# Unused bytes ahead of six SBUF pools of a three-layer transformer kernel

## The chip, the cores and the metric

One core of one Trainium2 chip runs the program. The time is the device time of one execution in microseconds; of several runs the median is taken.

## What is computed

A sequence of 512 tokens with 1,024 features goes through two layers of a first block and one of a second, all in float32. Cut to its outline:

```python
def first_block(x, ...):
    for layer in range(2):
        h = _rms_norm(x, norm_mix_pre[layer])
        m = _even_mixer(h, ...) if layer % 2 == 0 else _odd_mixer(h, ...)
        x = x + _rms_norm(m, norm_mix_post[layer])
        h = _rms_norm(x, norm_ffn_pre[layer])
        f = _conv_ffn(h, ...)          # gate, val = split(h @ w_up); (gelu(conv(gate)) * val) @ w_down
        x = x + _rms_norm(f, norm_ffn_post[layer])
    return x

def second_block(x, ...):
    x = x + gated_deltanet(rms_norm(x, norm_mix[0]), ...)
    x = x + squared_relu_mlp(rms_norm(x, norm_mlp[0]), ...)   # square(relu(h @ w_up)) @ w_down
    return rms_norm(x, norm_final)
```

The even mixer has eight heads of attention with a forget gate and eight of latent attention; the odd mixer has eight heads of differential attention; the DeltaNet is a gated delta rule in chunks of 64. Each mixer ends in a product with a 1024x1024 matrix `w_out`. The FFN is 2,816 wide, the MLP 4,096.

## The kernel before

A float32 product is computed as three products of parts. Every activation and every weight `v` is split into `hi` (rounded to the type float32r) and `lo = v - hi`, and `mm3` (lines 173 to 175) adds `hi*hi`, `hi*lo` and `lo*hi` in one PSUM bank:

```python
mm(out, lhs[0], rhs[0], start=start, stop=False)
mm(out, lhs[0], rhs[1], start=False, stop=False)
return mm(out, lhs[1], rhs[0], start=False, stop=stop)
```

`lhs` is the operand that is loaded into TensorE (128 columns of 4 bytes, 512 bytes of a partition); `rhs` streams past it (512 columns, 2,048 bytes). In the trace's names `out<-rhs,lhs` the streaming operand comes first.

Weights come in tiles of 128x1024: SyncE's queue loads `raw` (`wload`, line 153), ScalarE writes `whi` (line 168), VectorE or GpSimd `wlo` (line 169). The pool `wp` holds two `raw`, four `whi` and four `wlo`. The normed input of a layer lies transposed in `hhi` and `hlo` (pool `hp`). Two forms of product occur. In the first the weights are loaded and the activations stream (`step_A`: tiles `gate`, `val`, `up`, `dproj`, `kq`, `fkq`, `uq`, `kn`, `head`). In the second the activations are loaded and the weights stream (`proj_B`: `tok`, `headb`, `z`, `c`, `mv`; and `Out.mm`: `o`).

`Out` and `proj_out` compute the product that ends each mixer, FFN and half of the MLP. Its activation parts are `fhi`/`flo` and `mhi`/`mlo` (even mixer), `ahi`/`alo` (FFN), `ohi`/`olo` (odd mixer), `gp0` to `gp3` (DeltaNet) and `mhi`/`mlo` (MLP). For each 128 rows of the weight the loop goes over two halves of 512 columns and four token tiles, so that eight PSUM banks called `o` are filled, three matmuls in a row to a bank. The last four weight tiles (the tail) are taken token tile by token tile, so that norm and transposition (`pn_t`) of the next layer can begin; the order there is written by hand (`manual_schedule`), as it is in the two attention mixers.

Pools are opened and closed in program order, and a pool's tiles lie one behind the other in SBUF in the order in which they are first made. A tile that takes bytes which an earlier tile had waits for the earlier one's readers (`reuse_waits="tile"`). `conv_ffn` first makes `cw` (352 bytes of a partition) and loads it through SyncE's queue (line 1178), then makes `ahi` and `alo`.

Of the kernel before, what the change touches and what calls it, by code (L numbers as in the profile page):

```python
# [10 lines left out]
F32 = mybir.dt.float32  # L11
# [10 lines left out]
P = 128  # L22
# [42 lines left out]
def parts(hi, lo):  # L65

    return lambda k, t: (hi[:, k, t * P:(t + 1) * P], lo[:, k, t * P:(t + 1) * P])


class Kern:  # L70
# [41 lines left out]

    def pool(self, name, **kw):
        return self.tc.tile_pool(name=name, bufs=1, reuse_waits="tile", **kw)

    def ps(self, tag, name="ps"):

        return self.psum.tile([P, 512], F32, tag=tag, name=name, bufs=2)
# [323 lines left out]
    def even_mixer(self, gain_post, nxt):  # L442
        nc, a = self.nc, self.a
        with self.pool("ev_o") as op_:

            fox = op_.tile([P, 4, S], F32R, name="fhi"), op_.tile([P, 4, S], F32R, name="flo")
            oT = op_.tile([P, 4, S], F32, name="oT")
            act = [parts(*fox), None]
            out = Out(self, lambda k, t: act[k // 4](k % 4, t), 8, lambda k: a["ev_wout"][k])
            with self.pool("ev") as pp, self.smalls(pp):  # L450
                self._even_attention(pp, fox, oT, out)
            with self.pool("ev_w") as wo:
                mla = wo.tile([P, 4, S], F32R, name="mhi"), wo.tile([P, 4, S], F32R, name="mlo")
                act[1] = parts(*mla)
                for c in range(4):
                    self.split(mla[0][:, c, :], mla[1][:, c, :], oT[:, c, :])
                self.proj_out(out, self.postnorm_add(gain_post), nxt)

    def _even_attention(self, pp, fox, oT, out):
# [25 lines left out]


        qs, q2, k2 = [pp.tile([P, 2, S], F32R, tag=n, name=n) for n in ("qs", "q2", "k2")]
        cT = (pp.tile([P, 5, S], F32R, name="chi"), pp.tile([P, 5, S], F32R, name="clo"))
        low = (cT[0][:, 0:2, :], cT[0][:, 2:4, :]), (q2, k2)
        for q2, k2 in low:  # L490
# [378 lines left out]
    def odd_mixer(self, gain_post, nxt):  # L869
        nc, a = self.nc, self.a  # L870
        with self.pool("od_o") as op_:
            ohi = op_.tile([P, 8, S], F32R, name="ohi")
            olo = op_.tile([P, 8, S], F32R, name="olo")
            with self.pool("od") as pp, self.smalls(pp):
                out = Out(self, parts(ohi, olo), 8, lambda k: a["od_wout"][k])
                self._odd_attention(pp, ohi, olo, out)
            self.proj_out(out, self.postnorm_add(gain_post), nxt)
# [296 lines left out]
    def conv_ffn(self, l, gain_post, nxt):  # L1174
        nc, a = self.nc, self.a
        with self.pool(f"ff{l}") as pp:
            cw = pp.tile([P, NFF, 4], F32, name="cw")
            nc.sync.dma_start(cw, a["ff_conv"][l])
            ahi = pp.tile([P, NFF, S], F32R, name="ahi")
            alo = pp.tile([P, NFF, S], F32R, name="alo")  # L1180
            for j in range(NFF):
                if j == 0:
                    first = self.head_rest()
                if j < 2:
                    pg, pv = first[2 * j:2 * j + 2]
                else:
                    pg, pv = self.ps("a", "gate"), self.ps("b", "val")
                    for i, ps in enumerate((pg, pv)):
                        self.proj_A(ps, self.wtile(a["ff_wup"][l, 2 * j + i]), P, KC, self.hT)
                c = pp.tile([P, S], F32, tag="cv", name="cv", bufs=2)  # L1190
                nc.scalar.activation(c, pg, AF.Identity, bias=cw[:, j, 3:4], scale=cw[:, j, 2:3])
                for sft in (1, 2):
                    nc.vector.scalar_tensor_tensor(c[:, sft:], pg[:, :S - sft], cw[:, j, 2 - sft:3 - sft], c[:, sft:],
                                                   ALU.mult, ALU.add)
                nc.scalar.activation(c, c, AF.Gelu_apprx_tanh)
                nc.vector.tensor_tensor(c, c, pv, ALU.mult)
                self.split(ahi[:, j, :], alo[:, j, :], c)

            self.proj_out(Out(self, parts(ahi, alo), NFF, lambda k: a["ff_wdown"][l, k]), self.postnorm_add(gain_post), nxt)


    def deltanet(self, nxt):
        nc, a = self.nc, self.a
        self.spill_x()
        with self.pool("dn_o") as op_:

            wq = [op_.tile([P, 8, 4, 64], F32, tag=f"wq{t}", name=f"wq{t}") for t in range(NT)]
            new_parts = lambda t: op_.tile([P, 2, 8, P], F32R, tag=f"wq{t}", name=f"gp{t}")
            nw = op_.tile([P, 1], F32, name="dnw")
            nc.sync.dma_start(nw, a["dn_nw"])  # L1210
            with self.pool("dn") as pp, self.smalls(pp):
                hd = [dict(h=h, wq=[w[:, h] for w in wq]) for h in range(8)]
                with self.pool("dn_t") as tp:
                    st = {}
                    gates = self._dn_gates(tp, pp, st)
                    next(gates)
                    for n in ("lk", "lrho", "nk", "ikd"):
                        st[n] = pp.tile([P, 8, NT], F32, name="d" + n)

                    st["u"] = pp.tile([P, NT, 8, P], F32, name="u")  # L1220
                    st["rq"] = pp.tile([P, NT, 8], F32, name="rq")
                    for d in hd[:KA]:
                        self._dn_kq(tp, st, d)
                    for _ in gates:
                        pass
                    for h in range(8):
                        if KA <= h + 1 < 8:
                            self._dn_kq(tp, st, hd[h + 1])
                        self._dn_qk(tp, pp, st, hd[h])
                    solve = self._dn_solve(tp, st)  # L1230
                    next(solve)
                    for d in hd:
                        self._dn_v(tp, pp, st, d)
                        for _ in range(4):
                            next(solve, None)
                    for _ in solve:
                        pass
                with self.pool("dn_s") as sp:
                    out = self._dn_tail(sp, pp, st, hd, new_parts, nw)
            self.reload_x()  # L1240

            self.proj_out(out, self.plain_add(), nxt)
# [429 lines left out]
    def mlp(self, nxt):  # L1672
        nc, a = self.nc, self.a
        with self.pool("mlp") as pp:
            for part in range(2):
                hi = pp.tile([P, 16, S], F32R, tag="mhi", name="mhi", bufs=1)
                lo = pp.tile([P, 16, S], F32R, tag="mlo", name="mlo", bufs=1)
                for j in range(0, 16, 2):
                    if part + j == 0:
                        first = self.head_rest()  # L1680
                    if part == 0 and j < 4:
                        pss = first[j:j + 2]
                    else:
                        pss = [self.ps("ab"[i], "up") for i in range(2)]
                        for i, ps in enumerate(pss):
                            self.proj_A(ps, self.wtile(a["ml_wup"][part * 16 + j + i]), P, KC, self.hT)
                    for i in range(2):
                        r = pp.tile([P, S], F32, tag="relu", name="relu", bufs=3)
                        nc.scalar.activation(r, pss[i], AF.Relu)
                        nc.vector.tensor_tensor(r, r, r, ALU.mult)  # L1690
                        self.split(hi[:, j + i, :], lo[:, j + i, :], r)

                self.proj_out(Out(self, parts(hi, lo), 16, lambda k: a["ml_wdown"][part * 16 + k]), self.plain_add(),
                              nxt if part else None)
# [191 lines left out]
```

## Time and profile before

| | |
|---|---|
| median of 3 runs | 1962.18 us (1961.23 to 1965.1) |
| profiled execution, its own time | 1961.64 us |
| its span | 1959.9 us |
| granted TensorE clock, mean | 0.999 |
| TensorE busy | 1929.2 us, 98% of the span, 9,960 matmuls |
| weight loads | 1583.7 us, 81% |
| VectorE / ScalarE / GpSimd busy | 1012.9 / 819.2 / 253.2 us |
| DMA | 177.76 MB, mean 91 GB/s |

The span runs from the first to the last instruction of the profiled execution; the execution's own time is 1.74 us longer. Matmuls are pipelined: a matmul's duration in a row reaches from its start to its modelled end, and the next one starts long before that end. Busy time is the union of these durations.

### The profile page before, as it was taken

Reading aid. Unit: us, or ns where it says so; the run is one execution under the profiler, and the core shown is the slowest. Engines: PE = TensorE matmul, PEld = TensorE weight load, DVE = VectorE, ACT = ScalarE, POOL = GpSimd, SP = SyncE. Lnnn points to the kernel's source line nnn. Section 1 sums busy time; section 2 is a strip of 40 time slices with the busy share of each in tenths; the row PEclk is TensorE's granted clock in tenths of the full one; section 3 lists DMA queues with packets and bytes.
Section 4 is the critical chain, followed back from the end, with each engine's and each line's share of the span. In section 5 each row is a group of like instructions: output and inputs, shape, how many; then the busy total and the mean of one; then the engine's idle time right before and its main releaser. Section 6 shows DMA issues by size and latency. Waiting matters only on the chain.

```text
span 1959.9 us, 25300 instructions
## 1 busy us (share of the span) xinstructions
PE 1929.2 (98%) x9960; PEld 1583.7 (81%) x9960; DVE 1012.9 (52%) x1665; ACT 819.2 (42%) x1411; POOL 253.2 (13%) x336
## 2 busy tenths in 40 slices
PE   8999999999999999999999999999999999999998
PEld 6787688888888788878888888888788888888886
DVE  5666665444323647756444422677754655324423
ACT  4656544333312546744333321486532334313322
POOL 0213320000000324311000000100453310000000
PEclk9999999999999999999999999999999999999999
DMA  4112133333332321224333323332320233323322
GB/s 172 60 57 73 44 109 108 97 97 97 97 97 75 127 65 55 65 65 132 97 97 98 97 95 97 123 95 87 99 87 14 73 109 119 95 88 98 97 96 76
DMA packets 51643, 177.76 MB, mean 91 GB/s; under 512 B 7188, under 2 KB 8084, under 8 KB 51396
## 3 DMA queue, kind: packets, MB, share of 16 engines
q1 hardware_dynamic: 50068, 173.38, 27.8%
q0 software_dynamic: 1456, 2.76, 0.5%
q8 instruction: 79, 1.29, 0.3%
q14 instruction: 40, 0.33, 0.0%
HBM read 170.28 MB, written 5.77 MB: 90 GB/s over the span
## 4 chain that ended last, share of the span: by engine, by line
PE 52%; DVE 2%; ACT 1%; issue 1%; DMA 1%; POOL 0%; POOLq 0%; ACTq 0%; DVEq 0%
PE o L173 6%; PE o L175 6%; PE o L174 6%; PE up L173 3%; PE up L174 3%; PE up L175 3%; PE gate L174 2%; PE val L174 2%; PE val L175 2%; PE gate L175 2%; PE gate L173 2%; PE val L173 2%; PE dproj L173 2%; PE dproj L174 2%; PE dproj L175 2%
## 5 line engine op out<-in xcount | busy, mean ns | idle before, releaser
L169 DVE TENSOR_TENSOR wlo<-raw,whi 128x1024 fp32r<-128x1024 f32 (+1 forms) x277 | 341.0, 1232 | 552.0 <-ACT whi L168 547.5
L168 ACT CAST whi<-raw 128x1024 fp32r<-128x1024 f32 (+1 forms) x301 | 314.0, 1044 | 620.1 <-PE o L175 283.9
L173 PE MATMUL o<-whi,ahi 128*128 128x512 f32 x352 | 139.4, 396 | 0.0
L174 PE MATMUL o<-wlo,ahi 128*128 128x512 f32 x352 | 139.0, 395 | 0.0
L175 PE MATMUL o<-whi,alo 128*128 128x512 f32 x352 | 139.0, 395 | 0.0
L174 PE MATMUL gate<-hlo,whi 128*128 128x512 f32 x320 | 124.5, 389 | 0.0
L173 PE MATMUL gate<-hhi,whi 128*128 128x512 f32 x320 | 124.5, 389 | 0.0
L175 PE MATMUL val<-hhi,wlo 128*128 128x512 f32 x320 | 124.5, 389 | 0.0
L175 PE MATMUL gate<-hhi,wlo 128*128 128x512 f32 x320 | 124.5, 389 | 0.0
L173 PE MATMUL val<-hhi,whi 128*128 128x512 f32 x320 | 124.5, 389 | 0.0
L174 PE MATMUL val<-hlo,whi 128*128 128x512 f32 x320 | 124.5, 389 | 0.0
L173 PE MATMUL o<-whi,mhi 128*128 128x512 f32 x288 | 113.8, 395 | 0.0
L175 PE MATMUL o<-whi,mlo 128*128 128x512 f32 x288 | 113.6, 395 | 0.0
L174 PE MATMUL o<-wlo,mhi 128*128 128x512 f32 x288 | 113.6, 395 | 0.0
L188 POOL TENSOR_TENSOR po_rr<-po_ru,mhalf 128x1 f32<-128x1 f32 x16 | 8.7, 541 | 762.4 <-DVE po_ru L187 762.4
L175 PE MATMUL up<-hhi,wlo 128*128 128x512 f32 x224 | 87.3, 390 | 0.0
L173 PE MATMUL up<-hhi,whi 128*128 128x512 f32 x224 | 87.2, 389 | 0.0
L174 PE MATMUL up<-hlo,whi 128*128 128x512 f32 x224 | 87.2, 389 | 0.0
L175 PEld LDWEIGHTS o<-whi,alo 128*128 128x128 f32 x352 | 66.0, 187 | 16.2
L174 PEld LDWEIGHTS o<-wlo,ahi 128*128 128x128 f32 x352 | 66.0, 188 | 16.0
L173 PEld LDWEIGHTS o<-whi,ahi 128*128 128x128 f32 x352 | 66.0, 187 | 15.9
L174 PE MATMUL head<-hlo,whi 128*128 128x256 f32 (+1 forms) x256 | 72.3, 284 | 0.0
(414 smaller groups left out, 4411.0 us busy)
## 6 DMA issues: line engine op xcount, KB each, us to landing
raw<-in_ff_wup SPq DMA_DIRECT2D x88, 512.0 KB, 3.5
raw<-in_ff_wdown SPq DMA_DIRECT2D x44, 512.0 KB, 3.5
raw<-in_ml_wup SPq DMA_DIRECT2D x32, 512.0 KB, 3.5
raw<-in_ml_wdown SPq DMA_DIRECT2D x32, 512.0 KB, 3.5
raw<-in_dn_wqkv SPq DMA_DIRECT2D x24, 512.0 KB, 3.6
raw<-in_od_wqk SPq DMA_DIRECT2D x16, 512.0 KB, 3.5
raw<-in_ev_wqk SPq DMA_DIRECT2D x8, 512.0 KB, 3.5
raw<-in_ev_wout SPq DMA_DIRECT2D x8, 512.0 KB, 3.5
```

What stands on the lines that cost most here:

```text
L168: self.nc.scalar.copy(hi[:, :n], raw[:, :n])
L169: return (hi, lo), lambda: (eng or self.nc.vector).tensor_tensor(lo[:, :n], raw[:, :n], hi.bitcast(F32)[:, :n], ALU.subtract)
L173: mm(out, lhs[0], rhs[0], start=start, stop=False)
L174: mm(out, lhs[0], rhs[1], start=False, stop=False)
L175: return mm(out, lhs[1], rhs[0], start=False, stop=stop)
L188: nc.gpsimd.tensor_tensor(r, u, self.mhalf.to_broadcast([P, w]), ALU.pow)
```

## The change

Six pools get an unused tile, `pad`, made before the activations' parts: 384 bytes of each partition at the head of the even mixer's outer pool, the odd mixer's outer pool, the DeltaNet's outer pool and the MLP's pool; 480 bytes in the even mixer's inner pool; 32 bytes in FFN 0 and 288 in FFN 1, behind `cw`.

```diff
--- before.py
+++ after.py
@@ -112,6 +112,10 @@
 
     def pool(self, name, **kw):
         return self.tc.tile_pool(name=name, bufs=1, reuse_waits="tile", **kw)
+
+    def pad(self, pool, nbytes):
+
+        pool.tile([P, nbytes // 4], F32, name=f"pad{nbytes}")
 
     def ps(self, tag, name="ps"):
 
@@ -442,6 +446,7 @@
     def even_mixer(self, gain_post, nxt):
         nc, a = self.nc, self.a
         with self.pool("ev_o") as op_:
+            self.pad(op_, 384)
 
             fox = op_.tile([P, 4, S], F32R, name="fhi"), op_.tile([P, 4, S], F32R, name="flo")
             oT = op_.tile([P, 4, S], F32, name="oT")
@@ -485,6 +490,7 @@
 
 
         qs, q2, k2 = [pp.tile([P, 2, S], F32R, tag=n, name=n) for n in ("qs", "q2", "k2")]
+        self.pad(pp, 480)
         cT = (pp.tile([P, 5, S], F32R, name="chi"), pp.tile([P, 5, S], F32R, name="clo"))
         low = (cT[0][:, 0:2, :], cT[0][:, 2:4, :]), (q2, k2)
         for q2, k2 in low:
@@ -869,6 +875,7 @@
     def odd_mixer(self, gain_post, nxt):
         nc, a = self.nc, self.a
         with self.pool("od_o") as op_:
+            self.pad(op_, 384)
             ohi = op_.tile([P, 8, S], F32R, name="ohi")
             olo = op_.tile([P, 8, S], F32R, name="olo")
             with self.pool("od") as pp, self.smalls(pp):
@@ -1176,6 +1183,7 @@
         with self.pool(f"ff{l}") as pp:
             cw = pp.tile([P, NFF, 4], F32, name="cw")
             nc.sync.dma_start(cw, a["ff_conv"][l])
+            self.pad(pp, 32 + 256 * l)
             ahi = pp.tile([P, NFF, S], F32R, name="ahi")
             alo = pp.tile([P, NFF, S], F32R, name="alo")
             for j in range(NFF):
@@ -1203,6 +1211,7 @@
         nc, a = self.nc, self.a
         self.spill_x()
         with self.pool("dn_o") as op_:
+            self.pad(op_, 384)
 
             wq = [op_.tile([P, 8, 4, 64], F32, tag=f"wq{t}", name=f"wq{t}") for t in range(NT)]
             new_parts = lambda t: op_.tile([P, 2, 8, P], F32R, tag=f"wq{t}", name=f"gp{t}")
@@ -1672,6 +1681,7 @@
     def mlp(self, nxt):
         nc, a = self.nc, self.a
         with self.pool("mlp") as pp:
+            self.pad(pp, 384)
             for part in range(2):
                 hi = pp.tile([P, 16, S], F32R, tag="mhi", name="mhi", bufs=1)
                 lo = pp.tile([P, 16, S], F32R, tag="mlo", name="mlo", bufs=1)
```

No instruction is added, removed or moved, on any engine; line numbers behind line 114 shift. What follows from the addresses of the two built programs is where a tile's bytes begin within 512 bytes (address modulo 512):

| tiles | before | after |
|---|---|---|
| `whi`, `wlo`, `hhi`, `hlo` | 224 | 224 |
| `ahi`, `alo` of FFN 0 | 192 | 224 |
| `ahi`, `alo` of FFN 1 | 192 | 480 |
| `mhi`, `mlo` (MLP and even mixer), `fhi`, `flo`, `ohi`, `olo`, `gp0` to `gp3` | 352 | 224 |
| `chi`, `clo` (parts read by `uq`, `kn`, `mv`) | 384 | 224 |
| `qs`, `ks`, `kl` of the odd mixer (scores `sc`) | 480 | 352 |
| `qs` and `ks` of the even mixer | 384 and 32 | 256 and 384 |

Steps within these tiles are multiples of 512 bytes, so a slice begins where its tile does. Two waits change with the addresses. Here is SyncE's queue with the semaphores that each entry waits for, at the start of FFN 0, before the change (`raw` takes weights, `cw` the convolution's taps, `gain` a norm's gains):

```order
L153 DMA raw<-in_ff_wup 128x1024 [waits DMAHW4_49,Pool_49]
L153 DMA raw<-in_ff_wup 128x1024 [waits DMAHW5_49,DVE_49]
L1178 DMA cw<-in_ff_conv 128x88 [waits PE_49]
L143 DMA gain<-in_g_post 128x1024 [waits DVE_49]
L153 DMA raw<-in_ff_wup 128x1024 [waits DMAHW6_49,DVE_49]
L153 DMA raw<-in_ff_wup 128x1024 [waits DMAHW7_49,Pool_49]
```

And the same place after the change:

```order
L157 DMA raw<-in_ff_wup 128x1024 [waits DMAHW4_49,Pool_49]
L157 DMA raw<-in_ff_wup 128x1024 [waits DMAHW5_49,DVE_49]
L1185 DMA cw<-in_ff_conv 128x88
L147 DMA gain<-in_g_post 128x1024 [waits DVE_49]
L157 DMA raw<-in_ff_wup 128x1024 [waits DMAHW6_49,DVE_49]
L157 DMA raw<-in_ff_wup 128x1024 [waits DMAHW7_49,Pool_49]
```

The load of `cw` no longer waits for a TensorE semaphore, since the bytes that it takes belonged to the unused tile of the even mixer's pool and not to `fhi`; at FFN 1 it is the same. All else on the queue stands as it stood.

## Rows read from the trace of the kernel before

**Rows 1.** The page: busy times; shares of the chain by engine and line.

```profile
PE 1929.2 (98%) x9960; PEld 1583.7 (81%) x9960; DVE 1012.9 (52%) x1665; ACT 819.2 (42%) x1411; POOL 253.2 (13%) x336
...
PE 52%; DVE 2%; ACT 1%; issue 1%; DMA 1%; POOL 0%; POOLq 0%; ACTq 0%; DVEq 0%
PE o L173 6%; PE o L175 6%; PE o L174 6%; PE up L173 3%; PE up L174 3%; PE up L175 3%; PE gate L174 2%; PE val L174 2%; PE val L175 2%; PE gate L175 2%; PE gate L173 2%; PE val L173 2%; PE dproj L173 2%; PE dproj L174 2%; PE dproj L175 2%
```

**Rows 2.** Groups by line and shape: count, busy us, mean ns, idle before.

```profile
L174 PE MATMUL o<-wlo,ahi 128*128 128x512 f32 x352 | 139.0, 395 | 0.0
...
L174 PE MATMUL gate<-hlo,whi 128*128 128x512 f32 x320 | 124.5, 389 | 0.0
...
L174 PE MATMUL o<-wlo,mhi 128*128 128x512 f32 x288 | 113.6, 395 | 0.0
...
L174 PE MATMUL up<-hlo,whi 128*128 128x512 f32 x224 | 87.2, 389 | 0.0
L174 PE MATMUL head<-hlo,whi 128*128 128x256 f32 x240 | 67.9, 284 | 0.0
...
L174 PE MATMUL kq<-hlo,whi 128*128 128x512 f32 x128 | 50.1, 392 | 0.0
...
L174 PE MATMUL uq<-clo,whi 128*128 128x512 f32 x24 | 9.5, 397 | 0.0
...
L174 PE MATMUL head<-hlo,whi 128*40 128x256 f32 x16 | 4.5, 281 | 0.0
```

**Rows 3.** One tile, 330 to 510: duration min/median/max, first and last start.

```profile
L173 PE MATMUL gate<-hhi,whi x130: 389/389/390, 335.2 to 510.0; 128*128 128x512 f32 x130
...
L173 PE MATMUL val<-hhi,whi x136: 389/389/390, 329.8 to 508.6; 128*128 128x512 f32 x136
```

**Rows 4.** The same of `tok` (676 to 698) and `headb` (642 to 660).

```profile
L173 PE MATMUL tok<-whi,hhi x24: 389/389/390, 682.1 to 697.8; 128*128 128x512 f32 x24
...
L173 PE MATMUL headb<-whi,hhi x16: 388/389/487, 645.1 to 659.6; 128*128 128x512 f32 x16
```

**Rows 5.** The same of `ahi` (FFN 0, FFN 1) and `mhi` (MLP).

```profile
L173 PE MATMUL o<-whi,ahi x136: 393/395/397, 530.0 to 624.5; 128*128 128x512 f32 x136
...
L173 PE MATMUL o<-whi,ahi x136: 393/395/397, 1145.0 to 1239.5; 128*128 128x512 f32 x136
...
L173 PE MATMUL o<-whi,mhi x80: 390/393/404, 1699.9 to 1755.0; 128*128 128x512 f32 x80
```

**Rows 6.** Stretches of 20 us: busy us of each engine (count), clock, DMA.

```profile
core 0: us, PE busy (x) PEld busy (x) DVE busy (x) ACT busy (x) POOL busy (x), PEclk, DMA share, GB/s
580.00:600.00 20.00, 20.00 (x88) 16.05 (x87) 3.81 (x4) 4.19 (x4) 0.00 (x0) 1.00 0.32 103
1720.00:1740.00 20.00, 20.00 (x88) 16.21 (x87) 4.84 (x4) 4.19 (x4) 0.00 (x0) 1.00 0.29 94
```

**Rows 7.** Timeline of TensorE from 714.4: start us, duration us, group.

```profile
714.42 0.39 PE L970 MATMUL sc<-kl,qs 128*128 128x512 f32 x1
...
714.87 0.39 PE L970 MATMUL sc<-kl,qs 128*128 128x512 f32 x1
715.10 0.39 PE L173 MATMUL kq<-hhi,whi 128*128 128x512 f32 x1
...
716.01 0.39 PE L174 MATMUL kq<-hlo,whi 128*128 128x512 f32 x1
```

**Rows 8.** The same from 822.5, first and last of seven.

```profile
822.50 0.39 PE L173 MATMUL kq<-hhi,whi 128*128 128x512 f32 x1
...
823.89 0.38 PE L392 MATMUL ptr<-ident,L 128*128 128x128 f32 x2
```

**Rows 9.** Timeline of SyncE's DMA issues at `cw`; TensorE's longest total wait.

```profile
275.21 1.41 SPq L153 DMA_DIRECT2D raw<-in_ff_wup  x2
276.67 0.42 SPq L1178 DMA_DIRECT2D cw<-in_ff_conv  x1
...
PE pn_t L224 <- DVE nrm L216: 12.6, 6, 7.8
```

## Prediction

> **What bounds the kernel now.** I read the page's busy times and its chain first. TensorE is busy 1929.2 of 1959.9 us, and what the chain shares out by engine is nearly all TensorE's; the three lines of `mm3` writing the tile `o`, the products of `proj_out` and of the hand-placed `out.mm` calls, have 6% of the span each, the largest share [rows 1]. The granted clock is 1.00 in the stretches of `o` [rows 6]. So a nanosecond off a matmul of these lines is a nanosecond off the span, unless something else becomes late.
>
> Next, the groups by shape. The same 128x512 matmul has a mean of 389 ns where it writes `gate` or `up`, and of 395 where it writes `o` [rows 2]. That is a latency, and matmuls overlap, so what counts is the distance between starts. In 330 to 510 us `gate` and `val` have 130 + 136 matmuls of line 173, first at 329.8 and last at 510.0; each stands for three, so one takes 180.2 / 265 / 3 = **0.2267 us** [rows 3]. With `ahi` as weights it is 94.5 / 135 / 3 = **0.2333** in both FFNs, with `mhi` 55.1 / 79 / 3 = **0.2325** [rows 5].
>
> The reader is to see that roles and shape do not explain this. `tok` has the same roles as `o` (`whi` moves, an activation part is loaded) and takes 15.7 / 23 / 3 = 0.2275. `headb` changes its PSUM bank after every three matmuls, as `proj_out` does, and still has a median of 389 [rows 4]. What is left is where operands lie: `gate`, `val`, `up`, `tok` and `headb` read both at byte 224 of a 512-byte line; `o` moves from 224 and loads from 192 (FFN) or 352 (the rest). 192 and 352 also differ from each other in the same loop: durations of 393 to 397 against 390 to 404 [rows 5].
>
> **A second observation** sets the size. Equal offsets do not give 0.2267 at once. The six `kq` matmuls from 822.50, at 224 both, take (823.89 - 822.50) / 6 = 0.232 [rows 8]; the seven starts from 714.42 to 716.01 are 0.227 apart [rows 7]. `kq` is cut into short pieces by scores and transposes, and its mean is 392 [rows 2]. I read this as a rhythm between the weight load and the stream beside it: at equal offsets it settles after some eight matmuls and then holds, at 192 or 352 it never settles.
>
> **The change part by part.** No instruction is added, removed or moved, and nothing changes size. What changes is addresses and two waits.
>
> *`proj_out` of FFN 0 (528 matmuls, 192 to 224).* 488 stand in one run that follows `gate` directly, so it starts settled; the last 40 lie between transposes. 488 x 0.0066 = 3.2 us, and about 0.1 for the rest: **3.3**.
>
> *FFN 1 (528, 192 to 480).* The parts do not come to 224 but 256 bytes beyond. No long run of the trace has that distance. Bounds: nothing gained, or the full 3.3; a loss is excluded only as far as the worst duration seen, 404 against 395. The nearest row is the one hand-over with exactly this distance: the scores read at 480, and at 715.10 `kq` at 224 takes over. The starts stay 0.22 to 0.23 apart across it [rows 7]. A settled rhythm that survives the distance of 256 speaks for 256 being as good as 0. I take **3.3**.
>
> *MLP (768, 352 to 224).* All lie in one run with `up`, without transposes: 768 x (0.2325 - 0.2267) = **4.4**.
>
> *Both mixers' and the DeltaNet's `o` (3 x 192, 352 to 224).* 576 x 0.0058 = 3.3 if all settled. About a third stand in short pieces (between fills and in the tails), where 0.232 is no gain: **2.2**, between 1 and 3.3.
>
> *`uq`, `kn`, `mv` (120, one operand from 384 to 224).* Pieces of 3 to 18, now 397 on average for `clo` [rows 2]: 0 to 0.8, I take **0.2**.
>
> *Odd attention.* Its scores go from 480/480 to 352/352; among themselves still equal, but `kq` stays at 224, so a hand-over that had the distance 256 gets 128. If 75 of its 512 matmuls fall from 0.2267 to the unsettled 0.232, that is **-0.4**. At worst every one of the 512 matmuls of scores and projections loses 14 ns (404 - 390): -7.2.
>
> *Other matmuls.* Two-pass f32 matmuls and transposes move too; most keep their distance, and I count nothing. If 1,000 of them moved by 1 ns it would be 1 us either way.
>
> *The two waits.* `cw`'s load no longer waits for TensorE. It went out at 276.67, right behind the loads of 275.21 that took 1.41 us [rows 9]: nothing was waited for. Cost and gain 0; queued behind it are `gain` and the weights of the third block, as before.
>
> *What is late next.* A weight tile feeds 24 matmuls, 5.6 us; in 20 us of `proj_out` VectorE works 3.8 us and ScalarE 4.2, and the DMA engines have a share of 0.32 [rows 6]. At 5.45 us per tile none of them is late. In the tails TensorE waits for `nrm` (12.6 us in all, 7.8 of them at the start) [rows 9]. VectorE's work there follows the last blocks, and if it doesn't move, the saving of five tails of 96 matmuls is lost: 5 x 96 x 0.006 = 2.9 at most. But those tails were mostly counted as unsettled, so I subtract **-0.2**.
>
> Sum: 3.3 + 3.3 + 4.4 + 2.2 + 0.2 - 0.4 - 0.2 = **12.8 us**. The profiled execution took 1961.64 for its span of 1959.9; it becomes 1948.8. The median shown is 0.54 higher, so I forecast **1949.3**.
>
> **A rule against it.** In proj_out the weight load of one matmul and the stream of another run side by side, and rows 3 and 5 differ by 6.6 ns with the offset alone. The Trainium skill, "TensorE: Matmul & The Clock Gate", Part 2 (What happens when you issue a matmul), holds that TensorE has two independent SBUF read ports, so that loading the next weights "doesn't steal SBUF read bandwidth from the running matmul"; the trace does not agree with it as far as long f32r runs go. By that rule the sum is zero and the time stays at 1962.
>
> **Rivals.**
> - *The distance of 256 isn't settled ground; only offsets equal modulo 512 are.* Then FFN 1 gains nothing: 12.8 - 3.3 = 9.5, time 1952.6. For it: no long run has shown 256. Against: rows 7.
> - *No change: the 6 ns belong to `proj_out` itself* (its eight banks, its order), and moving the parts does nothing: 1962. For it: `o` was never seen at 224. Against: `headb` and `tok` [rows 4], and two different rhythms in one loop [rows 5]. The rule above would give the same time.
> - *Slower: equal offsets make the two streams meet.* At 256 columns the heads at equal offsets have 284, those with a 40-column load at shifting offsets 281 [rows 2]; there equal is not the better. If `o` went to the worst duration of rows 5, 404 against 395 or 393, its 2,400 matmuls would cost 2,400 x 0.010 = 24 us: 1986. It decides from a distance of starts above 0.233. Against: every long run at 224/224 has 0.2267.
> - *Half of the gain comes back* as waits in tails, as unsettled pieces and as dearer odd scores (-2.9, 1 instead of 2.2, some us of the -7.2): about 1955.
>
> **How the numbers follow.** All parts as summed: 0.70, itself between 1946.5 (15.6 if every piece settles) and 1951. Only equality modulo 512: 0.15, 1952.6. Half comes back: 0.05. No change: 0.06. Slower: 0.04. The likeliest gives 1949.3; the range must reach the second case and add the 0.5 us by which executions differ: 1945.5 to 1954, which leaves out the last three cases and some edge, 2 in 10. Faster by over 0.2% (3.9 us, about what a measurement of this kernel can tell): 0.90; within: 0.06; slower: 0.04.
>
> **What would show it.** `o` with `ahi`, `alo`, `mhi`, `mlo` at a median duration of 389 and starts 0.2267 apart, in FFN 0, FFN 1 and MLP each for itself; FFN 1 still at 395 would make the second case true. `gate`, `up` and `tok` must not move. `kq` and the odd scores may be dearer by some ns. The prediction is wrong if `o` stays at 0.233 with equal offsets, or if TensorE gets new idle time before `o` or `pn_t`.

## The result and the profile after

The change takes **1950.55 us** in the median (1949.29 to 1953.07, four runs); the kernel before, run beside it, takes 1963.64 (1961.23 to 1965.5, four runs). The ratio is 0.9936, with a 95% interval of 0.9918 to 0.9953. Forecast were 1949.3, and 1945.5 to 1954. The profiled execution took 1951.35 us with a span of 1949.6, which is 10.3 us below the span before (1959.9).

The page of the kernel after, busy times and the chain's shares by engine and line:

```profile
PE 1918.1 (98%) x9960; PEld 1585.1 (81%) x9960; DVE 1010.9 (52%) x1665; ACT 819.1 (42%) x1411; POOL 254.1 (13%) x336
...
PE 53%; DVE 2%; ACT 1%; issue 1%; DMA 1%; POOL 1%; POOLq 0%; ACTq 0%; DVEq 0%
PE o L177 6%; PE o L179 6%; PE o L178 6%; PE up L179 3%; PE up L177 3%; PE up L178 3%; PE gate L178 2%; PE val L178 2%; PE gate L177 2%; PE val L177 2%; PE gate L179 2%; PE val L179 2%; PE dproj L177 2%; PE dproj L179 2%; PE dproj L178 2%
```

TensorE's busy time fell by 11.1 us with the same 9,960 matmuls, and the busy times of the other engines differ by 2 us at most. What became shorter stands in the groups by line and shape, which answer to [rows 2]:

```profile
L178 PE MATMUL o<-wlo,ahi 128*128 128x512 f32 x352 | 137.0, 389 | 0.0
...
L178 PE MATMUL gate<-hlo,whi 128*128 128x512 f32 x320 | 124.5, 389 | 0.0
...
L178 PE MATMUL o<-wlo,mhi 128*128 128x512 f32 x288 | 112.1, 389 | 0.0
...
L178 PE MATMUL up<-hlo,whi 128*128 128x512 f32 x224 | 87.2, 389 | 0.0
...
L178 PE MATMUL kq<-hlo,whi 128*128 128x512 f32 x128 | 50.2, 392 | 0.0
...
L178 PE MATMUL uq<-clo,whi 128*128 128x512 f32 x24 | 9.4, 393 | 0.0
```

`o` has the 389 ns of `gate` and `up`, which did not move; `kq` stayed at 392. The single tiles, which answer to [rows 5] (`ahi` in FFN 0, `ahi` in FFN 1, `mhi` in the MLP; minimum/median/maximum in ns, first and last start):

```profile
L177 PE MATMUL o<-whi,ahi x133: 389/389/389, 529.9 to 619.7; 128*128 128x512 f32 x133
...
L178 PE MATMUL o<-wlo,ahi x126: 389/389/389, 1144.6 to 1229.6; 128*128 128x512 f32 x126
...
L178 PE MATMUL o<-wlo,mhi x82: 389/389/389, 1689.8 to 1744.9; 128*128 128x512 f32 x82
```

The spread is gone: every one has 389. The distances of starts are 89.8 / 132 / 3 = 0.2268, 85.0 / 125 / 3 = 0.2267 and 55.1 / 81 / 3 = 0.2267 us. The second row is FFN 1, whose parts lie 256 bytes from the weights' offset.

Where the 10.3 us of span come from is read from the starts of each stage's first matmul in both traces. The stages with a difference of 0.2 us or more (negative is shorter after; "main" is `proj_out` up to the first `pn_t`; the first stage begins with the first matmul, the last one ends with the last):

| stage | before, us | after, us | difference |
|---|---|---|---|
| first matmul to first `fkq` | 36.40 | 36.94 | +0.54 |
| first `fkq` to first `c` | 72.46 | 72.11 | -0.36 |
| `uq`, `kn` to first `o` | 48.57 | 48.31 | -0.26 |
| even mixer, first `o` to `o` of `mhi` | 40.82 | 42.14 | +1.32 |
| even mixer, `o` of `mhi` to first `head` | 24.05 | 23.58 | -0.47 |
| FFN 0, main | 114.10 | 110.85 | **-3.25** |
| odd mixer's `o`, main | 45.83 | 45.29 | -0.54 |
| FFN 1, main | 114.10 | 110.84 | **-3.25** |
| FFN 1, first `pn_t` to first `dproj` | 37.30 | 36.69 | -0.62 |
| first `dproj` to first `z` | 147.89 | 148.64 | +0.75 |
| DeltaNet's `o`, main | 59.25 | 59.60 | +0.34 |
| its first `pn_t` to first `up` | 35.73 | 35.53 | -0.20 |
| MLP, first `o` to the end | 265.83 | 261.49 | **-4.35** |

The three long runs give 10.85 us. All the rest adds up to half a microsecond the other way, with one entry that is not small: +1.32 in the even mixer. The windows of the kernel after, two that answer to [rows 6] and one at this entry; the last row is the same stretch of the kernel before:

```profile
core 0: us, PE busy (x) PEld busy (x) DVE busy (x) ACT busy (x) POOL busy (x), PEclk, DMA share, GB/s
580.00:600.00 20.00, 20.00 (x90) 16.55 (x89) 4.90 (x4) 4.22 (x4) 0.00 (x0) 1.00 0.28 97
...
1720.00:1740.00 20.00, 20.00 (x90) 16.57 (x89) 4.90 (x4) 3.93 (x4) 0.00 (x0) 1.00 0.28 83
...
219.00:222.40 3.40, 3.40 (x12) 2.73 (x11) 1.87 (x9) 1.53 (x6) 0.00 (x0) 0.50 0.20 82
...
219.00:222.40 3.40, 3.40 (x23) 2.78 (x21) 2.20 (x10) 2.61 (x8) 0.00 (x0) 1.00 0.26 105
```

90 matmuls lie in 20 us of `proj_out` instead of 88 (each count takes in those that reach in from before). In 219.0 to 222.4 the granted clock is 0.50, the lower of TensorE's two levels (1.2 GHz), and 12 matmuls lie in it; the kernel before has 1.00 and 23 matmuls in the same stretch. Just before it TensorE waits 1.9 us for `P`, in the kernel before 1.8. Waits of TensorE after, and the last row before (us in total, times, longest):

```profile
PE pn_t L228 <- DVE nrm L220: 12.0, 5, 7.9
PE vt L1515 <- ACT v L1512: 3.1, 1, 3.1
PE sc L680 <- ACT P L420: 1.9, 1, 1.9
PE o L178 <- DVE wlo L173: 1.3, 2, 0.8
...
PE o L177 <- ACT whi L172: 0.5, 1, 0.5
PE head L179 <- POOL wlo L173: 0.5, 1, 0.5
...
PE o L174 <- DVE wlo L169: 0.9, 2, 0.5
```

`pn_t` waits 12.0 us in all, where it was 12.6 [rows 9]. Small waits are new or longer: `o` waits 0.4 us more for `wlo` and 0.5 for `whi`, all of it in the DeltaNet's `o`, and a `head` 0.5 for `wlo` in the tail of FFN 1. That is why the DeltaNet's stage is 0.34 longer although its starts lie closer (below).

### The profile page after: what moved, and what is told of

Same layout as the page of the kernel before. It is cut to its first block, busy times and chain, and to the rows that moved or that the text cites. A ratio compares the mean times of both kernels' runs of the same rounds, so it can differ in the third digit from the quotient of the medians.

```text
span 1949.6 us, 25300 instructions
## 1 busy us (share of the span) xinstructions
PE 1918.1 (98%) x9960; PEld 1585.1 (81%) x9960; DVE 1010.9 (52%) x1665; ACT 819.1 (42%) x1411; POOL 254.1 (13%) x336
## 3 DMA queue, kind: packets, MB, share of 16 engines
q8 instruction: 79, 1.29, 0.3%
## 4 chain that ended last, share of the span: by engine, by line
PE 53%; DVE 2%; ACT 1%; issue 1%; DMA 1%; POOL 1%; POOLq 0%; ACTq 0%; DVEq 0%
PE o L177 6%; PE o L179 6%; PE o L178 6%; PE up L179 3%; PE up L177 3%; PE up L178 3%; PE gate L178 2%; PE val L178 2%; PE gate L177 2%; PE val L177 2%; PE gate L179 2%; PE val L179 2%; PE dproj L177 2%; PE dproj L179 2%; PE dproj L178 2%
## 5 line engine op out<-in xcount | busy, mean ns | idle before, releaser
L179 PEld LDWEIGHTS o<-whi,alo 128*128 128x128 f32 x352 | 66.1, 188 | 13.7
L178 PEld LDWEIGHTS o<-wlo,ahi 128*128 128x128 f32 x352 | 66.1, 188 | 13.7
L179 PE MATMUL head<-hhi,wlo 128*128 128x256 f32 (+1 forms) x256 | 72.2, 283 | 0.5 <-POOL wlo L173 0.5
```

## The experiments

**1. Equal offsets before, taken apart.** The weights' pool of the kernel before gets 128 unused bytes, so that `whi` and `wlo` lie at 352 while `hhi` and `hlo` stay at 224. The later pools move by the same 128 bytes, so that `o` keeps its distances (the loaded operand begins 32 bytes short of the moving one in the FFNs, 128 beyond it in the MLP) at another place.

```diff
+        self.wp.tile([P, 32], F32, name="pad")
```

> The kernel before with 128 unused bytes ahead of the weights' pool: whi and wlo go from 224 to 352, hhi and hlo stay at 224, the activations' parts move with the weights (320 and 480), so o keeps its distances of -32 and 128. Theory A: gate, val, up and tok, which were at distance 0, get 128 and go from 0.2267 to 0.2325; some 3,600 dense matmuls by 5 to 5.8 ns are 18 to 20 us, so about 1.010 of the kernel before; o stays at 0.2333 and 0.2325. Rival D (the 6 ns belong to the loop of proj_out): nothing changes, ratio 1.000. Rival B (absolute place): o, now loaded from 320 and 480 and moving from 352, changes too.

Measured: 1981.02 us in the median against 1963.36, ratio 1.0088 (1.0071 to 1.0105). Tiles `gate` (330 to 510 us) and `ahi` (FFN 0) of this kernel:

```profile
L174 PE MATMUL gate<-hhi,whi x130: 390/393/404, 329.8 to 508.9; 128*128 128x512 f32 x130
...
L174 PE MATMUL o<-whi,ahi x129: 393/394/397, 534.7 to 624.3; 128*128 128x512 f32 x129
```

`gate` takes over the very durations that `o` with `mhi` had before, 390/393/404 [rows 5]; both load from 128 bytes beyond where the moving operand begins. The stage of `gate` and `val` grew from 217.63 to 223.09 us in each FFN. `ahi`, moved as a whole, kept (624.3 - 534.7) / 128 / 3 = 0.2333. So neither the loop of `proj_out` nor a place by itself makes the rhythm, but the distance of the two operands: the slow rhythm went into a loop of the other form by an address alone.

**2. Every distance, in one kernel.** At the end of the changed kernel 42 runs of 40 further products are appended, with the operands' offsets chosen for each run; they are pure extra work.

```diff
+            for r, (n, cols, m, d) in enumerate(runs):
+                ps = self.ps("ab"[r % 2], "bench")
+                for i in range(REP):
+                    j = m // 4 if m else (i % 2) * (1024 - n)
+                    k = d // 4 + 128 * (i % 4)
+                    nc.tensor.matmul(ps[:cols, :n], lo[:, k:k + cols], hi[:, j:j + n], start=i == 0, stop=i == REP - 1)
```

> The changed kernel with 42 runs of 40 extra matmuls behind its last product; they write two PSUM banks that nobody reads, so the span gets some 380 us longer. In each run the moving operand starts m bytes and the loaded one d bytes from the weights' offset. Theory A (what counts is the distance of the two operands modulo 256: at 0 the weight load and the stream beside it fall into a fixed rhythm): starts 0.2267 us apart at distances 0 and 256, also where both are moved together by 4 to 128 bytes, and 0.230 to 0.234 at every other distance from 16 to 480. Rival B (an absolute place, 224 modulo 256, is the good one): 0.2267 only while the loaded operand stays at 224 or 480, and both moved together is as slow as one moved alone. Rival C (modulo 512): 256 is as slow as 128. With 96, 64 or 32 loaded columns, A expects the difference between distances to shrink; with 256 moving columns 0.120 at distance 0 and something else elsewhere.

The tile `bench`, in the stretches of the runs with the operands 0, 32 and 256 bytes apart, and of both 4 bytes further (the last three rows have two or three matmuls of the neighbouring runs):

```profile
L1698 PE MATMUL bench<-whi,wlo x40: 387/389/504, 1942.4 to 1951.4; 128*128 128x512 f32 x40
...
L1698 PE MATMUL bench<-whi,wlo x42: 392/395/398, 1979.0 to 1988.6; 128*128 128x512 f32 x42
...
L1698 PE MATMUL bench<-whi,wlo x42: 389/389/397, 2062.6 to 2071.8; 128*128 128x512 f32 x42
...
L1698 PE MATMUL bench<-whi,wlo x43: 392/400/402, 2117.8 to 2127.8; 128*128 128x512 f32 x43
```

Distances of starts, worked out for every run from its 11th and its 40th start in the trace, in ns. The second line of numbers has the runs of experiment 6 at the same distances:

| distance, bytes | 0 | 4 | 8 | 16 | 32 | 64 | 96 | 128 | 160 | 192 | 224 | 240 | 256 | 288 | 320 | 384 | 448 | 480 |
|---|---|---|---|---|---|---|---|---|---|---|---|---|---|---|---|---|---|---|
| one run after another | 226.8 | 232.2 | 230.7 | 233.3 | 233.3 | 233.2 | 234.4 | 232.4 | 233.4 | 229.0 | 233.2 | 226.7 | 226.7 | 233.4 | 233.4 | 232.3 | 228.8 | 233.2 |
| each behind one at 128 | 226.7 | | 230.7 | 233.3 | | | | | | | 233.3 | 228.4 | 226.7 | | | | | |

So 256 is as good as 0, and 32, 64, 128, 192 and 224 give the times of 288, 320, 384, 448 and 480: what counts is the distance modulo **256**, for a loaded operand of 512 bytes. With the moving operand 128 bytes further and the loaded one 128 or 32 short of it or 128 beyond, the times are 232.3, 233.3 and 232.4, as the modulus asks. 4 and 8 bytes cost 5.4 and 3.9 ns, 16, 32 and 48 (233.3) as much as 64. Both operands moved together by 32, 64, 96 or 128 bytes give 226.7; by 4 bytes 237.7, by 16 bytes 229.9: the distance is not all, and at equal offsets it was the multiples of 32 that gave the best time. Loads of 96, 64 or 32 columns take 228.9 to 240.1 at 0, 32 and 128 bytes, and none of them 226.7. Their three distances lie 2.8, 1.7 and 9.5 ns apart, those of 128 columns 6.5: that a smaller load shrinks the differences held for 96 and 64 columns, not for 32. With 256 columns moving, 0 and 256 bytes take 120.0, 32 bytes 118.4, 64 bytes 117.8 and 128 bytes 118.6: there equal is the worst of those measured.

**3. Not all loads at one distance.** In the change `ahi` keeps its distance or gets 128, and `alo` gets 128 more than `ahi`; the MLP's parts go to 64.

```diff
-            self.pad(pp, 32 + 256 * l)
+            self.pad(pp, 32 + 128 * l)
             ahi = pp.tile([P, NFF, S], F32R, name="ahi")
+            self.pad(pp, 128)
...
-            self.pad(pp, 384)
+            self.pad(pp, 448)
```

> The changed kernel with other unused bytes: FFN 0 has ahi at distance 0 and alo at 128, FFN 1 has ahi at 128 and alo at 256, the MLP has both parts at 64. Theory A with a rhythm that needs many matmuls to settle: one odd load in three keeps it from settling, so both FFNs are near 0.230 to 0.233. Rival E (each load pays for its own distance alone): FFN 0 at (2 x 0.2267 + 0.2325) / 3 = 0.2286 and FFN 1 at (0.2267 + 2 x 0.2325) / 3 = 0.2306, with durations of 389 for the loads at 0 or 256. MLP at 64: 0.230 to 0.234 by A; 0.2267 if the distance counted modulo 64 or less. In all 5 to 10 us more than the changed kernel.

Measured: 1962.30 us in one run, span 1960.5; nearly the whole gain is gone: it is 11.8 us more than the change, where 5 to 10 were expected. `ahi` and `alo` of FFN 0 in its trace:

```profile
L177 PE MATMUL o<-whi,ahi x131: 389/389/389, 529.8 to 619.9; 128*128 128x512 f32 x131
L178 PE MATMUL o<-wlo,ahi x130: 396/396/396, 530.0 to 619.4; 128*128 128x512 f32 x130
...
L179 PE MATMUL o<-whi,alo x130: 397/397/397, 530.2 to 619.7; 128*128 128x512 f32 x130
```

One load in three has another distance, and all three take turns in a rhythm of (619.9 - 529.8) / 130 / 3 = 0.2310 us, two thirds of the way back to 0.2333. FFN 1, with two loads in three at 128, keeps nothing, and the MLP at 64 is slower than before the change:

```profile
L177 PE MATMUL o<-whi,ahi x129: 393/393/393, 1144.9 to 1234.5; 128*128 128x512 f32 x129
...
L177 PE MATMUL o<-whi,mhi x79: 393/398/398, 1699.9 to 1754.5; 128*128 128x512 f32 x79
```

These are 89.6 / 128 / 3 = 0.2333 us and 54.6 / 78 / 3 = 0.2333. Against the kernel before, the stages of FFN 0, FFN 1 and the MLP differ by -1.08, +0.01 and +0.69 us. Rival E asked for 0.2286 and 0.2306 in the FFNs and for 389 ns wherever a load lies at 0 or 256; the second row of FFN 0 lies at 0 and has 396. A matmul doesn't take its own distance's time: the three of a group set one rhythm.

**4. The odd scores put back.** The change, with 128 more bytes in the odd mixer's inner pool, so that `qs`, `ks` and `kl` lie at 480 as before.

```diff
+                self.pad(pp, 128)
```

> The changed kernel with 128 more unused bytes in the odd mixer's inner pool, which puts the scores' operands at 480 again, 256 from the projections' 224. Theory A: hand-overs between scores and projections keep the rhythm again, kq and sc as in the kernel before, worth 0.2 to 0.5 us in the odd mixer and nothing elsewhere. Rival (the scores' offset doesn't matter): the odd mixer takes what it takes in the changed kernel within 0.1 us.

Measured: 1951.23 us in one run, span 1949.5. The stage from the first `sc` to the first `o` of the odd mixer takes 123.80 us, with the scores at 352 (the change) 124.01, before the change 123.98. The difference of 0.2 us says nothing: in four other traces with the scores at 352 (experiments 2, 3, 6 and the second kernel of 5) the stage takes 123.81 to 124.26. No effect of the scores' place is seen, and the change itself lost nothing there.

**5. The two halves of the change.** One kernel keeps the unused bytes of the FFNs and the MLP alone. Against the change, with the first line taken out of the even mixer, the odd mixer and the DeltaNet:

```diff
-            self.pad(op_, 384)
-        self.pad(pp, 480)
```

The other keeps those of the mixers and the DeltaNet alone:

```diff
-            self.pad(pp, 32 + 256 * l)
-            self.pad(pp, 384)
```

> Only the FFNs (both 288 bytes in FFN 1 and 32 in FFN 0, as in the change) and the MLP keep their unused bytes; the even mixer, the odd mixer and the DeltaNet lie as before. Theory A (only the long runs of o win, the mixers' pieces give nothing): FFN 0 -3.25, FFN 1 -3.25, MLP -4.35, so -10.9 us in sum, ratio 0.9945, and the mixers' stages as before within 0.1. Theory B (the prediction's sum: the mixers carry 2.2 + 0.2 - 0.4): the same three stages, and a ratio 2 us worse than the whole change, 0.9945 against 0.9935. Theory C (the mixers lose, +1.3 in the even, +0.75 before z): -10.9 and a total 1 to 2 us better than what those stages would give with the change. If A holds, this kernel is as fast as the change within 0.1%.

> Only the mixers' and the DeltaNet's unused bytes are kept; FFNs and MLP lie as before. Theory A (pieces between transposes and fills never settle): 0 within 0.7 us, ratio 1.000; stages of the even mixer's two forms of o, of odd proj_out (-0.5) and of the DeltaNet's gp as in the change, summing to 0. Theory B (the prediction's terms): -2.0 us, ratio 0.9990. Theory C (the mixers lose): +1 to +2, ratio 1.0007. FFN 0, FFN 1 and MLP must stay at starts of 0.2333 and 0.2325 (393 to 395 ns in duration).

Measured: FFNs and MLP alone 1950.63 us (five runs), ratio 0.9936 (0.9922 to 0.9950); mixers alone 1961.92 (eleven runs), ratio 0.9993 (0.9984 to 1.0002), beside 1963.05 for the kernel before (fifteen runs). The times tell no difference between the first and the whole change. Its stages have -3.25, -3.25 and -4.35, to 0.01 us what the change has, and +0.07, +0.01, +0.07 and +0.36 in the four with `o` of the mixers, whose bytes did not move. The second has 0.00 in the first three and -0.29, -0.51, -0.38 and -0.32 in the four. Its ratio leaves room for the 2.0 us of theory B and for none. `ahi` in FFN 0 of the second:

```profile
L177 PE MATMUL o<-whi,ahi x129: 393/394/397, 530.3 to 619.9; 128*128 128x512 f32 x129
```

Its even mixer lies where that of the change lies, and shows what the +1.32 was. The stretch of the clock's fall, in the windows of the second:

```profile
219.00:222.40 3.40, 3.40 (x24) 2.67 (x24) 2.12 (x8) 2.42 (x8) 0.00 (x0) 1.00 0.11 45
```

The clock is 1.00 here, behind the same wait of 1.9 us for `P`, and the stage is 0.29 us shorter than before, not 1.32 longer. The loss belongs to the clock's fall, and the fall does not come with the unused bytes alone.

What the mixers' bytes do to the starts themselves can be read apart from such losses. Of the mixers' `o`, 497 neighbouring starts lie less than 260 ns apart both before and in the change. Their mean distance falls from 232.4 to 227.9 ns, which is 2.21 us in all: 0.28 and 0.47 in the even mixer, 0.70 in the odd one, 0.75 in the DeltaNet. Counted in the same way it is 2.26 in the second kernel and nothing in the first.

In the first kernel the stage from `dproj` to `z` is 1.29 us longer than before (in the change 0.75). TensorE's waits between 1255 and 1430 us of the first:

```profile
PE vt L1511 <- ACT v L1508: 2.8, 1, 2.8
PE kt L1454 <- ACT kq L1450: 0.9, 1, 0.9
```

Before the change no wait for `kq` is seen here; now it is 0.9 us (in the change 0.2). TensorE comes out of FFN 1's tail 0.6 us early in both, but that this makes `kq` late is not shown: the second kernel waits 0.2 us for it too, and its tail of FFN 1 is as long as before.

**6. Is it 0 and 256 alone?** As experiment 2, with twenty distances, each behind a run at 128 bytes.

```diff
+            for d in DIST:
+                runs += [(512, 128, 0, 128), (512, 128, 0, d)]
```

> The change, with 40 runs of 40 products 128x512 appended, in pairs: one run at a distance of 128 bytes (never settles, 232.4 ns), then one at the distance asked for: 0, 8, 16, 80, 112, 144, 176, 208, 216, 224, 232, 236, 240, 244, 248, 252, 256, 264, 272, 496. Theory A (a settled rhythm is reached from any start at 0 and 256 alone; what 240 showed was a rhythm kept from the run before): 0 and 256 begin unsettled and settle within some ten products at 226.7; 240 stays at 228 or more; 16, 272, 496 and the rest 228 to 234. Theory B (240, that is 16 short of 256, is as good as 256 by itself): 240 and 496 settle at 226.7. Theory C (a window of distances below 256 is good): 232 to 252 all 227. Any distance below 226 would be a better place than the change's.

The tile `bench` at 216, 240 and 252 bytes:

```profile
L1695 PE MATMUL bench<-whi,wlo x42: 389/389/396, 2102.0 to 2111.3; 128*128 128x512 f32 x42
...
L1695 PE MATMUL bench<-whi,wlo x42: 387/392/395, 2176.1 to 2185.4; 128*128 128x512 f32 x42
...
L1695 PE MATMUL bench<-whi,wlo x42: 389/389/398, 2231.8 to 2241.1; 128*128 128x512 f32 x42
```

0 and 256 start at 228, 233, 231 and 236, 228, 233, 230 ns and hold 226 to 227 from the fourth and the fifth on. But 216 and 252 have 226.7 as well, 240 had 226.7 in experiment 2 and 228.4 here, 496 (which is 240 modulo 256) has 226.7; and 232, 236, 244 and 248 between them have 231.1, 231.8, 233.3 and 233.3. Of the rest, 80, 112, 144, 176 and 208 have 230.0 to 233.5, and 264 and 272 the 230.7 and 233.3 of 8 and 16. None of the three theories holds: the best rhythm is reached at 0 and 256 each time, at some distances below 256 too, and at 240 in one run of two. Why 240 differs is not shown; the run before it was at 224 in experiment 2 and at 128 here. No distance is below 226.6.

## Why the prediction was right, and where it wasn't

**What bounds the kernel, and the reading of the offset: right.** A nanosecond off a matmul of the long runs was a nanosecond off the span. That the place and not the loop is the cause is shown by experiment 1, which put the slow rhythm into `gate`, and by experiment 2, which changed nothing but the place. The rule of the Trainium skill, "TensorE: Matmul & The Clock Gate", Part 2 (What happens when you issue a matmul), by which loading the next weights takes no read bandwidth from the running matmul, would have left the time at 1963. The traces of long f32r runs do not agree with it: a shift of 128 bytes alone cost 17.7 us in experiment 1.

**FFN 0 (3.3), FFN 1 (3.3), MLP (4.4): right to 0.1 us each** (3.25, 3.25, 4.35). For FFN 1 a hand-over of a few starts [rows 7] was all that spoke for a distance of 256, so that taking the whole 3.3 there was a bet; the run of 126 and the period of 256 in experiment 2 settle it, and the first rival (only modulo 512) falls with them.

**The mixers' `o` (2.2): right for the starts, not seen in the time.** The starts lie closer by 2.21 us (experiment 5), as the forecast had it. Of this the four stages, which leave out two of the tails, show 1.5 us in the kernel with the mixers' bytes alone, and 1.1 and 1.0 in experiments 2 and 6, whose mixers lie the same way. In the profiled execution of the change all of it is hidden, by the clock's fall in the even mixer and by the waits for `wlo` and `whi` in the DeltaNet. The wait of 0.8 us for `wlo` there does not come from the mixers' bytes, for it stands in experiment 1 and in the first kernel of experiment 5 too. By the medians, the whole change is no faster than FFNs and MLP alone (1950.55 and 1950.63), but runs that spread over 3 us and more do not resolve 1 or 2.

**`uq`, `kn`, `mv` (0.2): right** (0.26).

**The two waits (0): right.** SyncE's DMA issues of the kernel after at `cw`, which answer to [rows 9]:

```profile
276.11 1.41 SPq L157 DMA_DIRECT2D raw<-in_ff_wup  x2
277.57 0.42 SPq L1185 DMA_DIRECT2D cw<-in_ff_conv  x1
```

`cw` goes out right behind the loads that take 1.41 us, as before; nothing was waited for, and nothing is gained.

**The odd attention (-0.4): wrong, no loss is seen.** The stage changed by 0.02 us. The step that failed is that a hand-over from 352 to 224 costs a rhythm that was there: `kq` had 392 ns before and has 392 after, and the mean distance of its neighbouring starts was 230.2 ns and is 230.1. It was largely unsettled already.

**What is late next (-0.2 for the tails): too small for the execution that was profiled, and at other places.** FFN 0's tail did not change (0.11 us longer). FFN 1's gained 0.62, but only 0.10 in experiment 6 with the same bytes there. The losses lie in the DeltaNet: 0.9 us of waits in its `o`, and 0.75 between `dproj` and `z`. Matmul by matmul, 0.1 of the 0.75 is lost up to 1359 us, the stretch that has the wait of 0.2 for `kq`, 0.3 more up to the end of the wait for `v`, which takes 3.1 us where it took 2.8, and the last 0.3 in a fall of the clock. The granted clock falls to 0.50 for 3.4 us here in both traces, at 1419.1 us before and at 1413.7 after; before, 0.6 us of that lay in the wait for `v`, after none. Since this stage is also 0.42 and 0.47 longer in the mixers' kernel and in experiment 3, whose tails of FFN 1 gained nothing, the loss is not shown to be what the tail had gained.

**The picture of the rhythm was too simple.** "At 192 or 352 it never settles" is wrong as a picture: there the starts repeat too, in a longer round (231, 235, 233, 234 ns at 192). And equality is not the only good place, as 216 and 252 show. At equal offsets the rhythm settled after three to twelve products in experiments 2 and 6, where the forecast had some eight. This cost the forecast nothing, since all the moves of `o` went to 0 or 256. How the engine makes these rounds stays open; the runs show at which distances, not by what.

**The other rivals.** No change, slower at equal offsets, and half of the gain coming back are excluded by the interval and by the stages. The heads that spoke for "slower" were read rightly: 256 columns do take longer at equal offsets (experiment 2), but 512 columns don't.

The gains added up to 13.4 and the losses to 0.6, which made 12.8. In the profiled execution the closer starts of `o` and of `uq`, `kn` and `mv` give 13.7 (3.42, 3.43, 4.38, 2.21 and 0.24, tails included), and the span shrank by 10.3: the losses were 3.4, of which the fall of the clock in the even mixer takes about 1.6 (1.32 instead of -0.29). The medians differ by 13.1, and the ratio's interval makes 9.2 to 16.1 of 1963.6, too wide to tell these apart. So the mechanism and the gains were right; that the medians come within 0.3 us of the sum is in part luck.

## What to carry to other kernels

When one shape of matmul has two mean durations in one kernel, compare where its two operands begin, not only what they are; for 128x512 products in f32r the loaded and the moving operand at the same offset modulo 256 bytes, both at a multiple of 32, were worth 2 to 3% of every long run. The gain is whole in runs without interruption (the mixers' pieces gave 2.2 us in their starts where full runs would have given 3.3, and less in time), and three loads that take turns must all be placed. For another shape it must be measured again, as 256 columns preferred another distance.

## What the runs showed of the hardware that was not expected

At a granted clock of 1.00 and equal offsets a 128x512 product takes 226.7 ns and a 128x256 product 120.0. The 256 columns more cost 106.7 ns, 0.417 each, which is one clock at 2.4 GHz; by this working both products have 13.3 ns beside their columns. The smaller one can do better at another distance (117.8), the larger was not seen to.

The starts repeat exactly over hundreds of matmuls, in rounds whose length depends on the distance; at 128 bytes two rounds were seen in one execution, of 232.4 and of 233.3 ns. The slower one stands behind the runs at 8, 112, 248, 252 and 264 bytes, so it seems that the run before decides.

The granted clock falls to 0.50 for 3.4 us behind one and the same wait of 1.9 us for `P` in one kernel and not in another with the same even mixer. It cost about 1.6 us. The same even mixer stands in the change, in experiments 2, 3, 4 and 6 and in the second kernel of 5; the fall came in the change and in experiments 3 and 4, not in the other three. Why, no run shows. In the DeltaNet the clock falls in every trace with a wait of 2.8 to 3.3 us for `v`, during the wait or up to 1.4 us behind it, for 3.4 us and in experiment 6 for 6.8. In experiment 1, the one trace without that wait, it does not fall there. Whoever compares stages of two executions has to look for these falls first.
